# Modulation products on 32-column tiles of TensorE, and attention over 512 keys at a time, in a two-layer hybrid encoder

## The chip, the cores and the metric
The kernel runs on one core of a Trainium2 chip. The metric is the device time of one execution in microseconds (us). The engines are TensorE (PE; its weight loads are listed as PEld), VectorE (DVE), ScalarE (ACT), GpSimd (POOL) and SyncE (SP), which issues most of the transfers.

## The reference, cut to what matters
The program computes two layers over 1024 tokens of width 1024. Each sub-layer is a norm, a shift and scale that come from a vector c, the sub-layer itself, a gate from c, and a residual add. Layer 0 mixes the tokens by S5 blocks and stick-breaking attention side by side; layer 1 by two recurrences. A mixture of 32 experts follows each. The change touches the modulation (all twelve vectors of both layers are computed inside layer 0) and the attention:

```python
def modulate(h, shift, scale):
    return h * (1.0 + scale[:, None, :]) + shift[:, None, :]

def stick_breaking_attention(q, k, v):
    ...
        z = jnp.einsum('bhqd,bhkd->bhqk', q[:, :, s0:s1], k[:, :, :s1]).astype(jnp.float32) * scale
        mask = jnp.arange(s1)[None, :] < jnp.arange(s0, s1)[:, None]
        log_keep = jnp.where(mask, jax.nn.log_sigmoid(-z), 0.0)
        rc = lax.cumsum(log_keep, axis=3, reverse=True)
        suffix = jnp.concatenate([rc[..., 1:], jnp.zeros_like(rc[..., :1])], axis=-1)
        w = jnp.where(mask, jnp.exp(jax.nn.log_sigmoid(z) + suffix), 0.0)
        outs.append(jnp.einsum('bhqk,bhkd->bhqd', w.astype(v.dtype), v[:, :, :s1]))
```

Each modulation vector is silu(c) (1024 numbers) times a 1024 x 1024 matrix, plus a bias. There are eight heads of 64; queries come in blocks of 128.

## The kernel before, in words
A tile framework records the program and a scheduler places each instruction in its engine's queue; each engine and each transfer queue then works strictly in that order. The order is therefore not the order of the code.

`even` (L1970 on) is layer 0. Its stages in time: the first four token tiles are normed while `ada` computes scale1 and shift1; the norm's result is modulated and split into two parts (hTh, hTl) whose three products stand for one of full precision; eight weight tiles are loaded (`wl`), split (`wsplit`) and multiplied (`proj_u`, `proj_qk`, `proj_v`, by `mm3`, L240 to L242); then the loop over four S5 blocks (`s5_quad`) and eight attention blocks (`stick`) runs; then the gated unit `glu`, the output rows (`out_rows`) and the routing (`out_route`). The expert weights (L941) are loaded by numbers that the routing computes.

`ada` (L142) computes a modulation vector. A matrix comes in four loads of 1 MB into a ring of weight buffers. VectorE multiplies each of the eight row groups of a load by its 128 values of silu(c) and adds them up (L160, L167), which leaves one sum per partition and column; TensorE then adds over the partitions by products with a column of ones (L179). One load of the first vector goes to TensorE in whole (L177). Two vectors are computed at the start, eight between the projections (the `todo` list) and two in the gated unit. The ring has four buffers; two serve the projections' weights and two the modulation's (`pick`).

`stick(i)` (L283) computes 128 queries against (i+1) x 128 keys, for four pairs of heads, in blocks of 256 keys from the last to the first. Per block: two matmuls for the scores (L297), two sigmoids by ScalarE, on the block that holds the diagonal two masks by GpSimd (L307), then a running product over the keys from the right, by a scan per head on VectorE (L313) whose start is copied from the block before (L311), a product by GpSimd (L315), transposes by TensorE, an eviction (L322) and the value matmuls (L326):

```python
for r in range(2):
    v.tensor_tensor_scan(P[:, r, 0:n][:, ::-1], keep[:, r, 0:n][:, ::-1], zero.to_broadcast([128, n]),
                         P[:, r, n:n + 1], op0=OP.mult, op1=OP.add)
g.tensor_tensor(w[:, :, 0:n], w[:, :, 0:n], P[:, :, 1:n + 1], op=OP.mult)
```

Of the kernel before, what the change touches and what calls it, by code (L numbers as in the profile page):

```python
# [21 lines left out]
D = 1024  # L22
# [14 lines left out]
class Core:  # L37
# [42 lines left out]
    def consts(self):  # L80
        nc, c = self.nc, self.const
        ji = c.tile([128, 128], I32, name="ji")
        nc.gpsimd.iota(ji, pattern=[[1, 128]], base=0, channel_multiplier=-1)
        self.ident = c.tile([128, 128], FT, name="ident")
        nc.vector.tensor_scalar(self.ident, ji, 0.0, None, op0=OP.is_equal)
        self.ustrict = c.tile([128, 128], BF, name="ustrict")
        nc.vector.tensor_scalar(self.ustrict, ji, 0.0, None, op0=OP.is_gt)
        self.ones_b = c.tile([128, 128], BF, name="ones_b")
# [12 lines left out]
        nc.scalar.activation(self.cs, cr, AF.Silu)  # L101
        self.mod_d = self.dram.tile([2, 6, D], FT, name="mod_d")
# [39 lines left out]
    def ada(self, i, names, pool, tag, on_pe=((),), pool_eng=False):  # L142
# [4 lines left out]
        for m, nm in enumerate(names):  # L147
# [5 lines left out]
            for h in range(4):  # L153
                w = self.wload(aw[i, :, j * D + h * 256:j * D + (h + 1) * 256], 8)
                if h in on_pe[m % len(on_pe)]:
                    parts.append(w)
                    continue
                acc = pool.tile([128, 256], FT, name="adacc", bufs=4)
                eng = nc.gpsimd if pool_eng else nc.vector
                eng.tensor_scalar(acc, w[:, 0, :], self.cs[:, 0:1], None, op0=OP.mult)  # L160
                for k in range(1, KD):
                    wk, ck = w[:, k, :], self.cs[:, k:k + 1]
                    if pool_eng:
                        eng.tensor_scalar(wk, wk, ck, None, op0=OP.mult)
                        eng.tensor_tensor(acc, acc, wk, op=OP.add)
                    else:
# [4 lines left out]
            for h, x in enumerate(parts):  # L171
                for q in range(2):
                    qs = slice(q * 128, (q + 1) * 128)
                    p = pc[:, 2 * h + q:2 * h + q + 1]
                    if h in on_pe[m % len(on_pe)]:
                        for k in range(KD):
                            nc.tensor.matmul(p, x[:, k, qs], self.cs[:, k:k + 1], start=(k == 0), stop=(k == KD - 1))  # L177
                    else:
                        nc.tensor.matmul(p, x[:, qs], self.ones_f[:, 0:1], start=True, stop=True)  # L179
# [103 lines left out]
    def stick(self, i, qT, kT, vt, sb, zero):  # L283
# [3 lines left out]
        W = 256  # L287
        py = self.psum("d")
        nkey = (i + 1) * 128
        for hp in range(4):  # L290
            prev = None
            blk = 0
            for s in reversed(range((nkey + W - 1) // W)):
                k0, n = s * W, min(W, nkey - s * W)
# [4 lines left out]
                keep = sb.tile([128, 2, W], FT, name="keep", bufs=4)  # L299
                nc.scalar.activation(keep[:, :, 0:n], pzz, AF.Sigmoid, scale=-0.125)  # L300
                w = sb.tile([128, 2, W], FT, name="sw", bufs=4)
                nc.scalar.activation(w[:, :, 0:n], pzz, AF.Sigmoid, scale=0.125)
                P = sb.tile([128, 2, W + 1], FT, name="sP", bufs=4)
                if prev is None:
                    for tl, fill in ((keep, 1.0), (w, 0.0)):
                        d = tl[:, :, n - 128:n]
                        g.affine_select(d, d, pattern=[[0, 2], [-1, 128]], compare_op=OP.is_gt, fill=fill,  # L307
                                        base=0, channel_multiplier=1)
                    v.memset(P[:, :, n:n + 1], 1.0)
                else:  # L310
                    v.tensor_copy(P[:, :, n:n + 1], prev[:, :, 0:1])  # L311
# [1873 lines left out]
```

## Time and profile before

| what | value |
|---|---|
| median of 3 runs | 3071.89 us (3069.78 to 3077.01) |
| the profiled execution's own time | 3069.93 us |
| its span on the core | 3068.1 us |
| mean granted TensorE clock | 0.902 |
| busy share of the span: PE, DVE, ACT, POOL | 87%, 58%, 37%, 27% |
| DVE products of the modulation (L167) | 161.1 us, 329 instructions |
| DVE scans of the attention (L313) | 132.9 us, 160 instructions |

The shares are means over a program whose stages have different limits, so they don't tell what a stage waits for. In a time line, a matmul's duration includes the time until its result is out, so its successor starts before it ends; the distance between two starts is its price. TensorE's clock has two levels, 1.2 and 2.4 GHz; a granted clock of 0.82 is a mean of the two over a stretch. A matmul of plain float32 operands appears as two records, one of the split operands as one.

### The profile page before, as it was taken

The numbers are of one execution on the slowest core, as the hardware profiler recorded it, in microseconds if no ns is written. First come the engines' busy times: TensorE is split into PE (matmuls) and PEld (weight loads), VectorE is DVE, ScalarE is ACT, GpSimd is POOL, SyncE is SP. The second block draws the span as 40 slices with busy tenths as digits, with TensorE's granted clock in tenths as the row PEclk, the third lists the DMA queues.
The fourth block names the chain that finished last, engine by engine and source line by source line (L and its number), as shares of the span: only waits on it lengthen the run. The fifth ranks groups of instructions, "written<-read, shape, count | busy, mean of one in ns | idle before, by whom it ended". The sixth has DMA issues, their size and how long they took to land. (4 is left out here: it accounts for less than half of the span.)

```text
span 3068.1 us, 39923 instructions
## 1 busy us (share of the span) xinstructions
PE 2656.4 (87%) x14357; PEld 1854.7 (60%) x14357; DVE 1792.6 (58%) x3211; ACT 1120.7 (37%) x1777; POOL 831.2 (27%) x1157
## 2 busy tenths in 40 slices
PE   4987688989699999995799999999978799998991
PEld 4776466647444466662677777777877444566660
DVE  7546999655633477664734555646547434556664
ACT  4311456432232345552433323323233223345451
POOL 5260755324211031101301533354105111111101
PEclk9998689989799999997898978886988799999996
DMA  8746220223588899997745322244443689999995
GB/s 279 178 124 198 63 59 15 90 68 105 211 338 324 351 368 407 376 389 256 260 138 176 110 77 78 67 121 103 107 125 119 242 348 365 369 362 396 388 385 239
DMA packets 345018, 672.82 MB, mean 219 GB/s; under 512 B 118591, under 2 KB 259935, under 8 KB 293104
## 3 DMA queue, kind: packets, MB, share of 16 engines
q1 hardware_dynamic: 272960, 611.23, 54.7%
q10 hardware_dynamic: 56752, 25.41, 3.0%
q0 software_dynamic: 15104, 33.58, 3.0%
q8 instruction: 115, 1.88, 0.3%
q14 instruction: 87, 0.71, 0.1%
HBM read 611.31 MB, written 79.79 MB: 225 GB/s over the span
## 5 line engine op out<-in xcount | busy, mean ns | idle before, releaser
L139 DVE TENSOR_TENSOR wlo<-w,whi 128x1024 fp32r<-128x1024 f32 x384 | 451.4, 1220 | 114.0 <-ACT whi L138 112.3
L138 ACT ACTIVATE whi<-w 128x1024 fp32r<-128x1024 f32 x384 | 390.5, 1054 | 237.1 <-PE ps_g L839 69.9
L240 PE MATMUL ps_b<-hTh,wh 128*128 128x512 f32 x608 | 259.3, 428 | 28.2 <-ACT cc L1382 12.5
L241 PE MATMUL ps_b<-hTl,wh 128*128 128x512 f32 x608 | 255.2, 420 | 0.0
L242 PE MATMUL ps_b<-hTh,wl 128*128 128x512 f32 x608 | 254.8, 419 | 0.0
L788 POOL DMA_INDIRECT xg<-h_d,tok x56 | 80.6, 1440 | 641.6 <-PE ps_t L106 617.1
L847 DVE TENSOR_TENSOR hs<-hs,ps_u 128x512 f32<-128x512 f32 x48 | 32.9, 685 | 263.3 <-PE ps_u L917 212.4
L794 POOL DMA_INDIRECT ye_d<-y,tab x48 | 71.9, 1497 | 421.8 <-DVE y L856 328.4
L167 DVE SCALAR_TENSOR_TENSOR adacc<-w,cs,adacc 128x256 f32<-128x256 f32 x329 | 161.1, 507 | 5.2
L139 DVE TENSOR_TENSOR wl<-w,wh 128x1024 fp32r<-128x1024 f32 x84 | 104.0, 1253 | 97.3 <-ACT wh L138 88.1
L240 PEld LDWEIGHTS ps_b<-hTh,wh 128*128 128x128 f32 x608 | 124.8, 206 | 55.9 <-ACT cc L1382 13.3
L846 ACT ACTIVATE hs<-ps_g 128x512 f32<-128x512 f32 x48 | 28.7, 598 | 325.0 <-PE ps_g L917 244.8
L313 DVE TENSOR_TENSOR_SCAN sP<-keep,sP,sbz 128x256 f32<-128x256 f32 (+1 forms) x160 | 132.9, 874 | 21.7 <-POOL keep L307 10.5
L917 PE MATMUL ps_g<-w,xh 128*64 128x512 f32 x512 | 143.5, 598 | 0.0
L133 POOL TENSOR_TENSOR rs<-rm,nhalf 128x1 f32<-128x1 f32 (+2 forms) x56 | 49.9, 892 | 344.9 <-DVE rm L131 293.2
L138 ACT ACTIVATE wh<-w 128x1024 fp32r<-128x1024 f32 x84 | 86.3, 1053 | 150.5 <-PE ps_b L241 132.4
L241 PEld LDWEIGHTS ps_b<-hTl,wh 128*128 128x128 f32 x608 | 124.7, 205 | 27.2 <-DVE hTl L139 0.3
L242 PEld LDWEIGHTS ps_b<-hTh,wl 128*128 128x128 f32 x608 | 123.9, 204 | 28.3 <-issue 0.4
L917 PE MATMUL ps_u<-w,xh 128*64 128x512 f32 x512 | 137.6, 595 | 0.0
L315 POOL TENSOR_TENSOR sw<-sw,sP 128x512 f32<-128x512 f32 (+1 forms) x80 | 101.1, 1265 | 132.6 <-DVE sP L313 57.3
L926 PE MATMUL ps_y<-w,hh 128*64 128x512 f32 x512 | 122.0, 598 | 2.2 <-ACT hh L921 2.2
L1699 POOL TENSOR_TENSOR T<-N,X 128x60 f32<-128x60 f32 (+24 forms) x248 | 87.1, 351 | 125.2 <-DMA N<-n_d 93.3
(709 smaller groups left out, 6177.9 us busy)
## 6 DMA issues: line engine op xcount, KB each, us to landing
w<-in_moe_w_gate_dram SPq DMA_DIRECT2D x128, 1024.0 KB, 14.7
w<-in_moe_w_up_dram SPq DMA_DIRECT2D x128, 1024.0 KB, 14.8
w<-in_moe_w_down_dram SPq DMA_DIRECT2D x128, 1024.0 KB, 13.4
w<-in_ada_w_dram SPq DMA_DIRECT2D x48, 1024.0 KB, 5.8
w<-in_odd_w_in_dram SPq DMA_DIRECT2D x26, 1024.0 KB, 5.7
cy<-ye_d SPq DMA_DIRECT2D x16, 1024.0 KB, 10.8
cx<-xm_d SPq DMA_DIRECT2D x29, 512.0 KB, 7.5
w<-in_even_w_in_dram SPq DMA_DIRECT2D x8, 1024.0 KB, 8.5
```

The source lines that it names most:

```text
L138: self.nc.scalar.activation(hi, x, AF.Copy)
L139: self.nc.vector.tensor_tensor(lo, x, hi.bitcast(FT), op=OP.subtract)
L167: eng.scalar_tensor_tensor(acc, wk, ck, acc, op0=OP.mult, op1=OP.add)
L240: nc.tensor.matmul(p, a[0], b[0], start=first, stop=False)
L241: nc.tensor.matmul(p, a[0], b[1], start=False, stop=False)
L242: nc.tensor.matmul(p, a[1], b[0], start=False, stop=last)
L313: v.tensor_tensor_scan(P[:, r, 0:n][:, ::-1], keep[:, r, 0:n][:, ::-1], zero.to_broadcast([128, n]), P[:, r, n:n + 1], op0=OP.mult, op1=OP ...
L315: g.tensor_tensor(w[:, :, 0:n], w[:, :, 0:n], P[:, :, 1:n + 1], op=OP.mult)
L788: nc.gpsimd.indirect_dma_start(out=xg, out_offset=None, in_=h_d[:], in_offset=bass.IndirectOffsetOnAxis(ap=tokc, axis=0), bounds_check=T - ...
L917: nc.tensor.matmul(ps[z][r], x[:, 4 * h + k, r], w[z][h][:, k, :], start=(h == 0 and k == 0), stop=(h == 1 and k == 3))
L926: nc.tensor.matmul(py[n][r], ht[:, f, r], w[2][f // 2][:, f % 2, two[n]], start=(f == 0), stop=(f == 3))
L1699: g.tensor_tensor(o, N[:, 0:j, j:j + 1].to_broadcast([128, j, w]), X[:, j:j + 1, c:8].to_broadcast([128, j, w]), op=OP.mult)
```

## The change
`ada` no longer uses VectorE for products. silu(c) is stored in a tile `csz` whose 32 columns per row group hold the values in the first and zeros in the others. Each row group k is multiplied by TensorE with these 32 columns as weights, into the partitions of column tile k mod 4; the two groups that share a tile are accumulated. Two loads fill one bank, which ScalarE evicts; the sums over partitions by ones remain. Eight of the vectors move from the projections into the loop over S5 and attention blocks, one ahead of each `stick`; all four ring buffers serve the projections' weights first, three loads ahead.

`stick` takes 512 keys at a time. On the diagonal block both heads are scanned by one instruction over 2(n+1) elements: a zero in `keep` and a one in the added operand `mid` between the heads restart the product. The product with the sigmoids, the transposes and the value matmuls stay at 256 keys. `keep` and `P` have two buffers instead of four, of double size, `sw` and `swT` three.

```diff
-                acc = pool.tile([128, 256], FT, name="adacc", bufs=4)
-                eng = nc.gpsimd if pool_eng else nc.vector
-                eng.tensor_scalar(acc, w[:, 0, :], self.cs[:, 0:1], None, op0=OP.mult)
-                for k in range(1, KD):
...
-                        eng.scalar_tensor_tensor(acc, wk, ck, acc, op0=OP.mult, op1=OP.add)
+            for h2 in range(2):
+                pa = self.psum(tag)
+                for h in (2 * h2, 2 * h2 + 1):
+                    w = self.wload(aw[i, :, j * D + h * 256:j * D + (h + 1) * 256], 8)
+                    for k in range(KD):
+                        q = 32 * (k % 4)
+                        nc.tensor.matmul(pa[q:q + 32, h % 2 * 256:h % 2 * 256 + 256], self.csz[:, k, :], w[:, k, :],
+                                         start=(k < 4), stop=(k >= 4), tile_position=(0, q))
+                acc = pool.tile([128, 512], FT, name="adacc", bufs=2)
+                nc.scalar.activation(acc, pa, AF.Copy)
...
-        W = 256
+        W = 512
...
+                keep, w, P = [sb.tile([128, 2 * (W + 1)], FT, name=x, bufs=b)[:, 0:2 * (n + 1)].rearrange("p (r n) -> p r n", r=2)
+                              for x, b in (("keep", 2), ("sw", 3), ("sP", 2))]
...
+                    for r in range(2):
+                        g.memset(keep[:, r, n:n + 1], float(r))
+                    x, y = (x.rearrange("p r n -> p (r n)")[:, ::-1] for x in (keep, P))
+                    v.tensor_tensor_scan(y, x, mid[:, W - n:W + n + 2][:, ::-1], 1.0, op0=OP.mult, op1=OP.add)
...
-                pick(0)
-                w = {0: wl(0)}
+                w = {n: wl(n) for n in range(3)}
...
-                    pick(1)
-                    for _ in range((0, 1, 1, 2, 2, 2, 0, 0)[n]):
-                        for x in late:
-                            list(x)
-                        i, nm = todo.pop(0)
-                        late = [self.ada(i, [nm], ap, "e")]
-                        next(late[0])
...
                     for i in si:
+                        for x in late:
+                            list(x)
+                        late = [self.ada(j, [nm], ap, "e") for j, nm in todo[:1]]
+                        todo = todo[1:]
+                        for x in late:
+                            next(x)
                         stick(i)
```

Three places show how the queues change. The first is the queue of SP in the projections (w: a ring buffer; u_d and u: the S5 inputs on their way through memory; g_d, yo: the S5 outputs). Before:

```order
L77 DMA w<-in_even_w_in_dram 128x8x256
L262 DMA u_d<-ut 1024x1x64
L77 DMA w<-in_ada_w_dram 128x8x256 x3
L77 DMA w<-in_even_w_in_dram 128x4x512 x2
L77 DMA w<-in_ada_w_dram 128x8x256 x4
L77 DMA w<-in_s_w_glu_dram 128x4x512
L77 DMA w<-in_ada_w_dram 128x8x256 x5
L77 DMA w<-in_s_w_glu_dram 128x4x512
L77 DMA w<-in_ada_w_dram 128x8x256 x10
L547 DMA u_2314<-u_d 32x4x128 x8
```

The same stretch after the change:

```order
L77 DMA w<-in_even_w_in_dram 128x8x256 x6
L255 DMA u_d<-ut 1024x1x64 x2
L77 DMA w<-in_even_w_in_dram 128x4x512
L255 DMA u_d<-ut 1024x1x64 x5
L77 DMA w<-in_even_w_in_dram 128x4x512
L255 DMA u_d<-ut 1024x1x64
L77 DMA w<-in_ada_w_dram 128x8x256 x4
L544 DMA u_1845<-u_d 32x4x128 x8
L580 DMA g_d<-yo 32x4x128 x4
```

The modulation's loads have left the projections but for four ahead of the first S5 input, and the gated unit's weights are no longer loaded here.

The second is VectorE's queue where the attention begins (adacc: the modulation's sums; hr, hi, bb, tp: tiles of an S5 block; sP: the scan's result). Before:

```order
L160 TENSOR_SCALAR adacc<-w,cs 128x256
L167 SCALAR_TENSOR_TENSOR adacc<-w,cs,adacc 128x256 x6
L160 TENSOR_SCALAR adacc<-w,cs 128x256
L180 TENSOR_TENSOR adao<-ps_e,adac 128x8
L167 SCALAR_TENSOR_TENSOR adacc<-w,cs,adacc 128x256 x8
L556 MEMSET hr 128x4
L557 MEMSET hi 128x4
L309 MEMSET sP 128x2 x4
L160 TENSOR_SCALAR adacc<-w,cs 128x256
L167 SCALAR_TENSOR_TENSOR adacc<-w,cs,adacc 128x256 x6
```

After the change:

```order
L143 TENSOR_TENSOR wl<-w,wh 128x1024 x10
L553 MEMSET hr 128x4
L554 MEMSET hi 128x4
L335 TENSOR_TENSOR bb_1733<-bl_1729,cfr 128x64
L335 TENSOR_TENSOR t_1735<-bl_1730,cfi 128x64
L335 TENSOR_TENSOR bb_1734<-bl_1730,cfr 128x64
```

The projections' splits are followed at once by the first S5 block's operations.

The third is TensorE's queue at the end of the attention (gyh, gyl, gwh, gwl: the gated unit's split operands; csz: the modulation's weights). Before, inside the gated unit:

```order
L240 MATMUL ps_e<-gyh_4979,gwh_4995 128x512
L241 MATMUL ps_e<-gyl_4980,gwh_4995 128x512
L242 MATMUL ps_e<-gyh_4979,gwl_4996 128x512
L326 MATMUL ps_d<-swT,v 64x128 x4
L106 MATMUL ps_a<-ident,sw 128x128 x4
L297 MATMUL ps_b<-kT,qT 128x256 x2
L240 MATMUL ps_e<-gyh_4985,gwh_4995 128x512
L241 MATMUL ps_e<-gyl_4986,gwh_4995 128x512
```

After the change, where the gated unit begins:

```order
L164 MATMUL ps_e<-w,csz 32x256 x8
L325 MATMUL ps_d<-swT,v 64x128 x4
L110 MATMUL ps_a<-ident,sw 128x128 x4
L291 MATMUL ps_b<-kT,qT 128x128 x2
L172 MATMUL ps_e<-ones_f,adacc 128x1 x4
L325 MATMUL ps_d<-swT,v 64x128 x4
L110 MATMUL ps_a<-ident,sw 128x128 x4
L325 MATMUL ps_d<-swT,v 64x128 x4
L110 MATMUL ps_a<-ident,sw 128x128 x2
L233 MATMUL ps_e<-gyh_4639,gwh_4663 128x512
L234 MATMUL ps_e<-gyl_4640,gwh_4663 128x512
```

Modulation products now stand among the last attention blocks, and the gated unit starts when their last score matmuls (L291) have been issued.

## Rows read from the trace of the kernel before
**Rows 1.** Busy time by stretch; each engine's busy us and instructions, then clock and transfers.
```profile
core 0: us, PE busy (x) PEld busy (x) DVE busy (x) ACT busy (x) POOL busy (x), PEclk, DMA share, GB/s
0.00:50.00 50.00, 22.35 (x97) 19.78 (x98) 34.20 (x75) 18.91 (x30) 28.67 (x21) 1.00 0.96 318
...
284.00:552.00 268.00, 198.21 (x1335) 139.73 (x1333) 246.66 (x436) 135.34 (x283) 157.18 (x149) 0.82 0.21 55
552.00:640.00 88.00, 81.91 (x452) 57.89 (x452) 57.07 (x95) 31.30 (x57) 23.13 (x23) 0.92 0.28 84
640.00:698.00 58.00, 49.58 (x215) 26.35 (x212) 25.68 (x40) 23.16 (x40) 15.84 (x25) 0.85 0.19 57
```
**Rows 2.** Time lines of DVE and PE ahead of the projections: start us, us, engine, line.
```profile
50.86 0.17 DVE L180 TENSOR_TENSOR shift<-ps_e,adac 128x8 f32<-128x8 f32 x1
...
60.40 1.22 PE L240 MATMUL ps_b<-hTh,wh 128*128 128x512 f32 x2 [9.58 <-ACT hTh L138]
```
**Rows 3.** Groups of PE, 60 to 285 us: busy us, mean ns, idle before.
```profile
L240 PE MATMUL ps_b<-hTh,wh 128*128 128x512 f32 x192 | 80.7, 423 | 15.7 <-ACT hTh L138 9.6 <-ACT c L383 3.6 <-ACT ut L261 2.5
...
L240 PE MATMUL ps_b<-wh,hTh 128*128 128x512 f32 x64 | 25.1, 395 | 0.0
L179 PE MATMUL ps_e<-ones_f,adacc 128*128 128x1 f32 x112 | 15.5, 253 | 9.0 <-DVE adacc L167 9.0
```
**Rows 4.** Time line of PE at the first and the last matmuls of the projections.
```profile
61.41 0.63 PE L241 MATMUL ps_b<-hTl,wh 128*128 128x512 f32 x1
...
283.74 0.39 PE L240 MATMUL ps_b<-wh,hTh 128*128 128x512 f32 x1
283.97 0.39 PE L241 MATMUL ps_b<-wl,hTh 128*128 128x512 f32 x1
...
284.51 0.70 PE L297 MATMUL ps_b<-kT,qT 64*128 64x256 f32 x2
```
**Rows 5.** Groups of DVE, 284 to 697 us.
```profile
L313 DVE TENSOR_TENSOR_SCAN sP<-keep,sP,sbz 128x256 f32<-128x256 f32 (+1 forms) x160 | 132.9, 874 | 21.7 <-POOL keep L307 10.5 <-ACT keep L300 9.8
L167 DVE SCALAR_TENSOR_TENSOR adacc<-w,cs,adacc 128x256 f32<-128x256 f32 x80 | 39.9, 520 | 0.6
L311 DVE COPY sP<-sP 128x2 f32<-128x2 f32 x48 | 19.0, 397 | 1.2 <-DVE sP L313 0.5
...
L160 DVE TENSOR_SCALAR adacc<-w,cs 128x256 f32<-128x256 f32 x11 | 6.9, 632 | 18.4 <-DMA w<-in_ada_w_dram 17.7 <-PE ps_e L179 0.7
```
**Rows 6.** The scan's line: durations in ns, least, median and most.
```profile
L313 DVE TENSOR_TENSOR_SCAN sP<-keep,sP,sbz x160: 448/736/1895, 309.5 to 668.1; 128x256 f32<-128x256 f32 x128, 128x128 f32<-128x128 f32 x32
```
**Rows 7.** Groups of POOL, ACT and PE in the attention, 284 to 697 us.
```profile
L315 POOL TENSOR_TENSOR sw<-sw,sP 128x512 f32<-128x512 f32 (+1 forms) x80 | 101.1, 1265 | 132.6 <-DVE sP L313 57.3 <-ACT sw L302 52.7 <-DVE sP L309 9.7
L307 POOL TENSOR_SCALAR_AFFINE_SELECT sw<-sw 128x256 f32<-128x256 f32 x32 | 26.5, 829 | 29.5 <-ACT sw L302 26.8 <-issue 2.2
...
L322 ACT ACTIVATE swT<-ps_a 128x512 f32<-128x512 f32 (+1 forms) x80 | 44.6, 558 | 124.6 <-PE ps_a L106 99.9 <-issue 7.1 <-DVE bb L338 6.5
...
L326 PE MATMUL ps_d<-swT,v 128*64 128x128 f32 x576 | 58.1, 324 | 14.6 <-ACT swT L322 14.1
```
**Rows 8.** Time lines of PE and PEld where two 64-column tiles alternate (layer 0's experts).
```profile
850.90 3.65 PE L917 MATMUL ps_g<-w,xh 128*64 128x512 f32 x16
854.38 2.74 PE L917 MATMUL ps_u<-w,xh 128*64 128x512 f32 x10
...
851.38 0.14 PEld L917 LDWEIGHTS ps_g<-w,xh 128*64 128x64 f32 x2 [0.29 <-issue]
```
**Rows 9.** Time line of PE at the first output rows and the first split output matmul.
```profile
684.61 3.60 PE L681 MATMUL ps_e<-w,gl 128*128 128x512 f32 x8
688.05 3.60 PE L681 MATMUL ps_e<-w,qT 128*128 128x512 f32 x8
...
698.49 0.79 PE L240 MATMUL ps_e<-wh,yh 128*128 128x512 f32 x1
```
**Rows 10.** Time line of SP's queue: the first expert weight.
```profile
805.11 0.37 SPq L941 DMA_DIRECT2D w<-in_moe_w_gate_dram  x1
```

More of the change, by code (lines that the diff above doesn't have):

```diff
@@ L146, in ada @@
         aw, ab = a["ada_w"], a["ada_b"]
-        for m, nm in enumerate(names):
+        for nm in names:
             j = order.index(nm)
@@ L170, in ada @@
             pc = self.psum(tag)
[L171 to L179, printed above, removed]
+            for n in range(KD):
+                nc.tensor.matmul(pc[:, n:n + 1], parts[n // 4][:, n % 4 * 128:n % 4 * 128 + 128], self.ones_f[:, 0:1], start=True, stop=True)
             nc.vector.tensor_tensor(o, pc[:, 0:KD], b, op=OP.add)
@@ L323, in stick @@
-                for b in range(nb):
-                    for r in range(2):
-                        h = 2 * hp + r
-                        nc.tensor.matmul(py[64 * r:64 * r + 64, hp * 128:(hp + 1) * 128], vt[:, s * 2 + b, h * 64:(h + 1) * 64],
-                                         wT[:, (r * nb + b) * 128:(r * nb + b + 1) * 128],
-                                         start=(blk == 0), stop=(blk == i))
-                    blk += 1
-                prev = P
+                    for r in range(2):
+                        v.tensor_tensor_scan(P[:, r, 0:n][:, ::-1], keep[:, r, 0:n][:, ::-1], mid[:, 0:1].to_broadcast([128, n]),
+                                             P[:, r, n:n + 1], op0=OP.mult, op1=OP.add)
@@ new lines, in stick @@
+                prev = P
+                for b0 in reversed(range(0, n // 128, 2)):
+                    m = min(2, n // 128 - b0)
+                    ks = slice(b0 * 128, (b0 + m) * 128)
+                    g.tensor_tensor(w[:, :, ks], w[:, :, ks], P[:, :, b0 * 128 + 1:(b0 + m) * 128 + 1], op=OP.mult)
+                    pt = self.psum("a")
+                    for r in range(2):
+                        for z in range(m):
+                            self.transpose(pt[:, (r * m + z) * 128:(r * m + z + 1) * 128], w[:, r, (b0 + z) * 128:(b0 + z + 1) * 128])
+                    wT = sb.tile([128, 512], FT, name="swT", bufs=3)
+                    nc.scalar.activation(wT[:, 0:256 * m], pt[:, 0:256 * m], AF.Copy)
+                    for z in range(m):
+                        b = k0 // 128 + b0 + z
+                        for r in range(2):
+                            h = 2 * hp + r
+                            first = k0 + n == nkey and b0 + 2 >= n // 128 and z == 0
+                            nc.tensor.matmul(py[64 * r:64 * r + 64, hp * 128:(hp + 1) * 128], vt[:, b, h * 64:(h + 1) * 64],
+                                             wT[:, (r * m + z) * 128:(r * m + z + 1) * 128],
+                                             start=first, stop=(k0 == 0 and b0 == 0 and z == m - 1))
@@ L2092, in even @@
                     for i in si:
+                        for x in late:
[4 more added lines that the diff above has]
+                            next(x)
                         stick(i)
+                for x in late:
+                    list(x)
             phasors.close()
```

72 lines of the change are left out of this document (23 added, 49 removed).

## The prediction
> **What bounds the kernel now.** I read the busy table by stretches first [rows 1], then the time lines at the seams of the first layer [rows 2, 9, 10], then the groups of instructions inside each stretch. Only the first layer up to its routing is touched. The first expert weight is issued at 805.11 us [rows 10], on a queue whose issue waits for the routing result, and everything behind hangs on that. So what the first 805 us lose or gain moves the end of the program one for one, give or take the second layer's reordering. Four stretches matter. **Start:** the modulation vector is ready at 50.86 us and the first projection matmul starts at 60.40 [rows 2]. **Projections:** 60.4 to 284.5 us [rows 2, 4], the stretch of the big matmuls, where TensorE should run freely and, as worked out below, doesn't. **Attention with the S5 blocks:** from 284 to 552 us VectorE is busy 246.7 of 268 us, 92%, while TensorE's clock is granted at 0.82: VectorE bounds it. **Gated unit and first output rows:** 552 to 698.5 us, no engine alone; the gated unit is woven into the last attention blocks, and the first split output matmul comes at 698.49 [rows 9].
>
> **Start (gain 9 us).** Eight weight loads of 1 MB feed the first two modulation vectors. Today VectorE multiplies seven of them, in a chain that ends with the last product shortly before 50.9. On TensorE the products no longer limit; the loads do. The queue must land 11.5 MB (six x tiles and a seventh, eight weights) before the last product. At the 318 GB/s of this stretch [rows 1] that is 36 us; 2 us of matmuls, one eviction, eight column sums and an add follow, near 4 us together. That is 40 instead of 50.9. I take 9, with bounds 3 (loads stretched by waits for the ring) and 12.
>
> **Projections (gain 31 us).** The 768 large matmuls (six groups, three of 192 and three of 64, one of each shown [rows 3]) start 0.23 us apart when nothing interrupts [rows 4]: 175 us. With 24 transposes (5 us) that makes 180 of the 224.1 us; 44 are lost. Of these, the 112 small column sums take about 13 us (15.5 of overlapping duration), waits for VectorE's product sums 9.0 [rows 3], other waits about 8, and the rest, 14 us, is the lower of the two clock levels, 1.2 instead of 2.4 GHz, at which TensorE is found behind such gaps: the third matmul after the wait before 60.40 lasts 0.63 us, one in a long run 0.39 [rows 2, 4]. The change takes the sums, their waits and about 9 us of slow clock out of this stretch: 31 us. Bounds: 14 if only waits and part of the sums go, 40 if all but the other waits go. VectorE's splits for the projections become free of a neighbour, and four ring buffers instead of two prefetch the weights; I cost both at nothing, since TensorE hides them.
>
> **Attention, gated unit, output (gain 68 us).** Today 284.5 to 698.5, 414 us. *VectorE.* Removed: modulation products 39.9 + 6.9 us; 32 of 48 one-column copies at 0.40 us, 12.7 [rows 5]; the memsets go to GpSimd. The scans: 160 instructions become 64 over the same 36,900 elements. From the medians of 0.736 us for 256 and the minimum 0.448 for 128 [rows 6], an element costs 2.25 ns and an instruction 0.16 us. So 64 scans take 93 us undisturbed, and 114 with the stretch that today's sum shows (132.9 against 108). That removes 19 to 40 us. Together 79 to 100 us of durations; as durations overlap by about 6%, some 75 to 95 of the 329 busy us in 284 to 698. About 214 us are left for attention and S5. *GpSimd* keeps 101 us of products and 48 of masks (one of their two rows shown) [rows 7], with some 45 for S5 and 64 one-column memsets: about 200. *ScalarE* saves on 32 fewer pairs of sigmoids and gains sixteen evictions of the size of today's 0.56 [rows 7]. *TensorE* keeps its attention work and gains eight modulations of 32 products. A 512-column product of two records takes 0.86 us (eight records in 3.44 us [rows 9]), so one of 256 columns 0.43. If four 32-column tiles run side by side, 256 of them cost 27 us; one after another, 110. The nearest row has two 64-column tiles: sixteen records in 3.48 us, 0.22 each, half of 0.43 [rows 8]. So tiles do run side by side, and I take 27.
>
> That makes three engines of 200 to 225 us, where today one of 247 set the pace. I therefore don't carry over VectorE's 92%; at 80% attention takes 214 / 0.80 = 268 us. The order puts the gated unit behind the last attention blocks instead of among them: 192 matmuls at 0.23 us, 44, plus 2 for its start. Then 64 records of output rows at 0.43 us [rows 9] with 4 for a slow start, 32. Sum 346 against 414. Bounds: 92% busy gives 233 and a gain of 103; TensorE with the serial price is the first rival.
>
> The rows show the weights of the paired tiles loaded in 0.14 us per pair inside a period of 0.43 [rows 8], while TensorE never stands still: the loads are hidden. The Trainium skill, "TensorE: Matmul & The Clock Gate", Part 3 (The mechanism), says a weight load overlaps running matmuls only when its row group differs; column tiles share theirs. By that rule 512 loads would add 0.07 us each, an estimate of 36 us of TensorE in the attention, and my sum would end about 20 us later, near 2984. The row contradicts it, so my sum goes by the row.
>
> The Trainium skill, "TensorEngine Tiling (Array Packing)", Key Properties, says that changing the tiling mode drains the engine. Some 50 changes, each at most the difference between a transpose's 0.33 us and its turn of 0.11, would be 11 us by that rule. It is spread over an engine that has that room here, and no row shows a drain by itself.
>
> **What could be late next.** The ring holds exactly one modulation's four weights, so each next load waits for TensorE to pass the product before it; behind it on the queue of SP stand the S5 inputs of the next block and, late, the gated unit's inputs and weights. I cost this at nothing, since the transfer queue is used to a fifth in this stretch [rows 1]; the cover is the 268 us of attention for 32 MB (100 us at the rate of the start). The keep and scan buffers shrink from four of 256 to two of 512 keys; that is the third case below.
>
> **Sum.** 9 + 31 + 68 = 108 us off the profiled execution's own 3069.9 us (span 3068.1 and 1.8 around it): 2962. The median of the runs is 2 us above that execution, so 2964.
>
> **Rivals.** *First: the 32-column tiles run one after another.* For it: no row shows four of them. Against it: the pair of rows 8. TensorE would have 198 us (284 to 552) plus a quarter of 178 (the three attention groups, one shown [rows 7]) plus 110, 352 us, and become the bound: 430 with gated unit and output, 16 worse than today there, and with the 40 of the first stretches 24 us faster: 3048. *Second: the engines overlap as today.* VectorE at 92% and the start at its best give 12 + 31 + 103: 2926. For it: GpSimd and VectorE slow each other less when the products are gone (a scan runs up to 1.895 us against 0.736 [rows 6]). Against it: GpSimd and TensorE have no slack to lend. *Third, slower: the chain of a block sets the pace.* A block of 512 keys goes through two pairs of matmuls (1.7 us), two sigmoids (about 1.1 each), two masks (0.7 and 0.8), a scan of 1026 elements (2.5), a product (1.3), transposes, eviction and value matmuls (0.6 each): near 10.5 us. With two keep buffers two blocks can be in flight, 5.2 us each, and 48 blocks need 252 us, inside my 268. Break-even with today lies at 414 + 40 - 78 = 376 us, 7.8 us a block. If only one block is under way at a time, it is 504 us: 128 slower, near 3200. For it: fewer, larger blocks and halved buffers, with two masks and two memsets in series on GpSimd ahead of the scan. Against it: S5 work and another head pair's block stand between on every queue.
>
> **How the numbers follow.** Forecast with its own spread 0.78; first rival 0.10; second 0.07; third 0.05. The range reaches to 2918 (second rival with 8 us of reordering in the second layer) and to 3008 (half of the serial price, smallest gains ahead). Above it lie the first and third rivals. About 0.2% is what a measurement can tell from no change: faster 0.92, same 0.03, slower 0.05.
>
> **What would show it.** Right: projections' first matmul near 50 us and attention's first near 245; modulation products starting about 0.11 us apart; VectorE below 90% in the attention; first split output matmul near 590; first expert load near 697. Wrong: product matmuls 0.2 us apart or more (first rival), VectorE above 90% (second), GpSimd or ScalarE waiting in turn for the scan with every engine under 70% (third), or the seam at 805 moved while the end did not.

## The result, and the profile after the change

The change makes the kernel slower: 3120.66 us (median of 4 runs, 3110.23 to 3126.25) against 3071.99, a ratio of 1.0151 with the interval 1.0122 to 1.018. Forecast was 2964. The profiled execution has a span of 3108.5 us.

Busy time by stretch of the changed kernel, to be read beside [rows 1]:

```profile
core 0: us, PE busy (x) PEld busy (x) DVE busy (x) ACT busy (x) POOL busy (x), PEclk, DMA share, GB/s
0.00:50.00 50.00, 24.51 (x200) 14.89 (x200) 8.13 (x25) 22.09 (x37) 32.43 (x23) 0.80 1.04 343
...
55.00:243.00 188.00, 183.08 (x797) 149.82 (x799) 38.31 (x123) 46.53 (x60) 57.84 (x178) 0.97 0.16 46
243.00:400.00 157.00, 113.09 (x855) 75.32 (x855) 112.38 (x153) 71.69 (x129) 99.22 (x133) 0.86 0.32 73
400.00:500.00 100.00, 75.64 (x545) 49.07 (x547) 59.53 (x75) 50.60 (x86) 52.49 (x61) 0.82 0.33 100
500.00:610.00 110.00, 86.89 (x762) 57.98 (x758) 51.20 (x64) 49.68 (x83) 41.63 (x56) 0.86 0.64 166
610.00:718.00 108.00, 95.89 (x465) 62.25 (x461) 28.92 (x39) 24.18 (x38) 7.01 (x13) 0.93 0.50 139
```

VectorE's busy time in the attention is 223 us, near the 214 that were forecast, but that is 61% of 367 us where 80% of 268 was forecast, and 92% before: the attention got longer all the same. No engine is at 90% there; TensorE, the busiest, has 276 us (75%). The time line of PE shows the seams (first projection matmul, first score matmul L291, gated unit, output rows, first split output matmul), and the products L164 among the last attention blocks:

```profile
55.17 1.22 PE L233 MATMUL ps_b<-hTh,wh 128*128 128x512 f32 x2 [10.97 <-ACT hTh L142]
...
242.87 0.70 PE L291 MATMUL ps_b<-kT,qT 64*128 64x256 f32 x4
...
542.67 2.77 PE L164 MATMUL ps_e<-w,csz 128*32 128x256 f32 x48
545.38 0.65 PE L325 MATMUL ps_d<-swT,v 128*64 128x128 f32 x6
...
556.09 1.94 PE L164 MATMUL ps_e<-w,csz 128*32 128x256 f32 x16 [6.09 <-DMA w<-in_ada_w_dram]
...
559.84 1.13 PE L291 MATMUL ps_b<-kT,qT 64*128 64x512 f32 x4
560.90 1.07 PE L164 MATMUL ps_e<-w,csz 128*32 128x256 f32 x16
561.90 0.66 PE L325 MATMUL ps_d<-swT,v 128*64 128x128 f32 x8
...
610.83 0.79 PE L233 MATMUL ps_e<-gyh,gwh 128*128 128x512 f32 x1
...
684.25 0.68 PE L678 MATMUL ps_e<-w,gl 128*128 128x512 f32 x1
...
718.03 0.48 PE L233 MATMUL ps_e<-wh,yh 128*128 128x512 f32 x1
```

Beside [rows 2, 4, 9]: the start gained 5.2 us (60.40 to 55.17), the projections 36.4 (224.1 to 187.7). The stretch from the first score matmul to the first split output matmul, the **attention stretch** below, grew from 414.0 to 475.2. The queue of SP, beside [rows 10]:

```profile
542.92 0.39 SPq L77 DMA_DIRECT2D w<-in_ada_w_dram  x1
...
569.10 20.05 SPq L77 DMA_DIRECT2D w<-in_ada_w_dram  x6
592.36 2.54 SPq L77 DMA_DIRECT2D w<-in_s_w_glu_dram  x2
...
825.81 0.37 SPq L938 DMA_DIRECT2D w<-in_moe_w_gate_dram  x1
```

The first expert weight comes 20.7 us later, the end of the span 40.4 us. The gated unit's weights are issued at 592.36, behind the modulation's loads, and its first matmul at 610.83 stands behind the last scores, not among the attention blocks.

Groups of PE from 243 to 718 us: the products are 45.0 us (ten vectors, two of them in the gated unit) and wait 18.8 for loads; the value matmuls wait 36.5 for ScalarE's evictions, 14.1 before [rows 7].

```profile
L325 PE MATMUL ps_d<-swT,v 128*64 128x128 f32 x576 | 57.5, 317 | 37.4 <-ACT swT L319 36.5 <-issue 0.6
...
L164 PE MATMUL ps_e<-w,csz 128*32 128x256 f32 x640 | 45.0, 414 | 18.8 <-DMA w<-in_ada_w_dram 18.8
...
L172 PE MATMUL ps_e<-ones_f,adacc 128*128 128x1 f32 x160 | 20.5, 253 | 0.8 <-ACT adacc L167 0.8
```

Groups of DVE in the same stretch, the scans, 93.1 us in place of 132.9 [rows 5]:

```profile
L303 DVE TENSOR_TENSOR_SCAN sP<-keep,sbm 128x514 f32<-128x514 f32 (+3 forms) x32 | 52.7, 1646 | 59.7 <-POOL sw L313 23.4 <-POOL keep L301 18.1 <-POOL keep L298 18.1
L307 DVE TENSOR_TENSOR_SCAN sP<-keep,sP,sbm 128x512 f32<-128x512 f32 x32 | 40.4, 1301 | 6.2 <-ACT keep L293 5.3
```

The waits of 243 to 610 us (who waits for whom, us, times, longest) go in a circle. VectorE waits for GpSimd, GpSimd for ScalarE, ScalarE for VectorE, and ScalarE and TensorE wait for each other:

```profile
ACT swT L319 <- PE ps_a L110: 67.8, 46, 6.8
...
PE ps_d L325 <- ACT swT L319: 36.5, 15, 8.9
...
POOL sw L313 <- ACT sw L294: 24.4, 6, 11.9
...
DVE sP L303 <- POOL sw L313: 23.4, 4, 8.4
ACT keep L293 <- DVE sP L303: 18.2, 8, 4.5
```

### The profile page after: what moved, and what is told of

The parts are those of the page before. It is cut to its first block, busy times and chain, and to the rows that moved or that the text cites. A ratio compares the mean times of both kernels' runs of the same rounds, so it can differ in the third digit from the quotient of the medians.

```text
span 3108.5 us, 40569 instructions
## 1 busy us (share of the span) xinstructions
PE 2688.3 (86%) x14969; PEld 1854.8 (60%) x14969; DVE 1585.6 (51%) x2678; ACT 1129.0 (36%) x1735; POOL 810.9 (26%) x1223
## 3 DMA queue, kind: packets, MB, share of 16 engines
q1 hardware_dynamic: 272960, 611.23, 53.5%
## 5 line engine op out<-in xcount | busy, mean ns | idle before, releaser
L785 POOL DMA_INDIRECT xg<-h_d,tok x56 | 73.2, 1308 | 658.0 <-PE ps_t L110 624.6
L110 PE MATMUL ps_t<-ident,xg 128*128 128x128 f32 (+1 forms) x448 | 75.6, 307 | 42.5 <-DVE wlo L143 31.3
L836 PE MATMUL ps_g<-wlo,xh 128*128 128x512 f32 x256 | 105.3, 411 | 7.8 <-DVE wlo L143 7.6
```

The source lines that it names most:

```text
L110: self.nc.tensor.transpose(out, in_, self.ident[:n, :n])
L836: nc.tensor.matmul(p, x[a][:, k, :], w(b, j)[:, ns], start=(first and a + b == 0), stop=(last and a == 1))
```

## The experiments

The seams of every profiled execution. "Stretch" is the attention stretch, behind it TensorE's and VectorE's busy time in it; the median stands beside that of the kernel before from the same session.

| run | first projection | first score | stretch | PE, DVE busy | first expert | median (before) |
|---|---|---|---|---|---|---|
| before | 60.4 | 284.5 | 414.0 | 330, 329 | 805.1 | 3072.0 |
| changed | 55.2 | 242.9 | 475.2 | 372, 252 | 825.8 | 3120.7 (3072.0) |
| e1 | 54.3 | 242.1 | 483.3 | 379, 296 | 833.2 | 3124.5 (3075.5) |
| e2 | 59.9 | 282.9 | 416.5 | 328, 303 | 806.1 | 3093.5 (3075.5) |
| e3 | 54.2 | 330.0 | 384.0 | 316, 249 | 820.5 | 3097.3 (3075.5) |
| e4, e4 again | 54.2 | 284.5 | 379.6 | 314, 250 | 770.6 | 3053.6 (3075.5) |
| e5 | 54.8 | 242.5 | 437.5 | 362, 251 | 786.9 | 3521.7 (3069.3) |
| e6 | 55.2 | 288.9 | 380.7 | 321, 259 | 776.0 | 3054.7 (3069.3) |
| e9 | 55.3 | 244.3 | 481.7 | 377, 258 | 833.1 | 3091.8 (3069.3) |
| e10 | 60.4 | 283.1 | 385.3 | 319, 277 | 774.8 | 3060.4 (3069.3) |
| e12 | 59.9 | 283.8 | 432.5 | 337, 322 | 822.9 | 3117.5 (3073.8) |
| e12b | 60.4 | 283.6 | 419.0 | 335, 318 | 809.0 | 3080.1 (3073.8) |
| e13 | 55.3 | 278.1 | 409.3 | 327, 327 | 793.9 | 3086.8 (3073.8) |
| l0_before | 60.2 | 288.2 | 421.7 | 331, 329 | 816.6 | 1492.5 (3082.7) |
| l0_after | 54.8 | 241.8 | 485.7 | 376, 253 | 834.7 | 1514.4 (3082.7) |
| f1 | 53.5 | 241.1 | 496.0 | 360, 356 | 844.2 | 3158.5 (3082.7) |
| f3 | 54.4 | 303.8 | 400.9 | 314, 286 | 811.4 | 3108.5 (3082.7) |
| g1 | 55.6 | 279.2 | 410.2 | 328, 323 | 796.1 | 3070.9 (3071.0) |
| g2 | 55.2 | 242.6 | 481.9 | 383, 271 | 831.5 | 3108.7 (3071.0) |

In the row of e4 the median is that of e4, the rest is from e4 again. The first layer of l0_before has the rows of before in the same order, and its stretch took 421.7 instead of 414.0; l0_after 485.7 instead of 475.2. Differences of a stretch under some 10 us say nothing. Nor does a whole time tell of the first layer, since the scheduler orders the second anew at nearly every edit.

TensorE's busy share of the stretch lies between 77 and 84% in every run but f1 (73%), VectorE's between 52 and 80%. The stretch follows TensorE's busy time more closely than VectorE's. That is seen across runs and shows no cause by itself; the experiments below move the work.

**One half of the change each.** e1 is the changed kernel with `stick` as before; e2 is the kernel before with the new `stick`:

```diff
-    def stick(self, i, qT, kT, vt, sb, zero):
...
-        W = 256
+    def stick(self, i, qT, kT, vt, sb, mid):
...
+        W = 512
```

> The modulation products on TensorE inside the attention, as in the changed kernel, but the attention at 256 keys with a scan per head and four buffers, as before. Theory A (place): the eight vectors stand in TensorE's queue of the attention, wait there for their loads and hold the gated unit's weights back; the 512 keys cost nothing. Then this run is as slow as the changed kernel, 3100 to 3140 us, and the stretch from the first score matmul to the first split output matmul stays at 450 to 490 us (475 in the changed kernel, 414 before). Theory B (blocks): 512 keys with two buffers instead of four make the chain of a block the pace; the products are harmless. Then that stretch falls to 350 to 400 us and the run takes 3000 to 3050 us.

> The attention at 512 keys with one scan on the diagonal, as in the changed kernel, but the modulation on VectorE between the projections, as before. Theory A (place): VectorE is relieved of some 30 us of scans and copies and TensorE gets nothing new: faster than before by 10 to 40 us, 3030 to 3062 us. Theory B (blocks): slower than before by 20 us or more, 3092 us and above, with the stretch from the first score matmul to the first split output matmul above 440 us.

The stretch was 483 with the products alone and 416.5 with the 512 keys alone: the loss belongs to the modulation's move, as theory A has it. But by theory A e2 was to be faster, and the 26 us of busy time that VectorE loses there bought nothing. Its median, 3093.5, is in theory B's range and slower by 0.7% (interval 0.5 to 0.9%), though its stretch is far under theory B's 440 and its first expert weight is at 806.1: that loss lies behind the first layer.

**The eight vectors elsewhere, or nowhere.** e3 puts them back between the projections, on TensorE. e4 leaves out their loads, products and sums.

```diff
-                        late = [self.ada(j, [nm], ap, "e") for j, nm in todo[:1]]
...
+                    for _ in range((0, 1, 1, 2, 2, 2, 0, 0)[n]):
...
+                        late = [self.ada(i, [nm], ap, "e")]
```

```diff
-            for h2 in range(2):
+            for h2 in range(0 if skip else 2):
```

> The changed kernel with the eight vectors put back between the projections (two buffers of the ring for them, two for the projections' weights, as before), still multiplied by TensorE. Theory A (place): the attention loses its products and the gated unit is woven into it again: its stretch falls from 475 to 380 to 410 us, the projections grow from 188 to about 215 to 235 us; 3010 to 3060 us. Theory B (blocks): the attention's stretch stays above 440 us and the run at 3100 us or more.

> The changed kernel without the loads, products and sums of the eight vectors in the attention (these vectors hold only their biases; that part of the computation is left out). It prices them: Theory A (place) expects the stretch from the first score matmul to the first split output matmul to fall from 475 to 350 to 380 us and the run to 2990 to 3030 us; Theory B (blocks) expects it to stay above 430 us, the run above 3070 us.

> The same kernel as in e4 (the eight vectors hold only their biases), for its profile. It tells what the attention with 512 keys takes with no modulation in it: e3, which has none there but the last two, measured 384 us from the first score matmul to the first split output matmul. If products, sums and loads of the eight are the whole excess, it is 375 to 395 us; the products alone (e5, 437.5) then cost some 50 us and the loads 38. If it is above 420, something else than the eight vectors holds the attention.

384.0 and 379.6 us: without modulation the attention takes 380. In e3 the projections grew to 275.8 us, 88 more than in the changed kernel and beyond the 235 expected, and the run took 3097.3 where 3010 to 3060 was expected: on TensorE the work costs there too. On VectorE, as before, it costs the projections 36 (224.1 against 187.7), and the attention stretch some 32 (e2 against e3), in which VectorE still multiplies eleven loads. The stretch of e4 in one row (columns as in the first view): TensorE is busy for 83% of it, VectorE for 66%.

```profile
284.50:664.10 379.60, 313.97 (x1983) 208.88 (x1982) 250.16 (x317) 186.76 (x319) 197.75 (x262) 0.91 0.19 57
```

Its whole time is no price, since its projections take 230 us, for another reason. With nothing ahead of them, the eight biases are copied early in VectorE's queue and wait there for their loads (waits of DVE, 55 to 130 us):

```profile
DVE adao L171 <- DMA adac<-in_ada_b_dram: 34.6, 5, 18.7
```

**Products or loads.** e5 multiplies the keys, which lie on the chip, instead of loaded weights; e6 loads the weights and leaves the products out.

```diff
-                    w = self.wload(aw[i, :, j * D + h * 256:j * D + (h + 1) * 256], 8)
...
+                        w = res[:].rearrange("p a (b n) -> p (a b) n", n=256)
```

```diff
+            if skip:
+                for h in range(4):
+                    self.wload(aw[i, :, j * D + h * 256:j * D + (h + 1) * 256], 8)
-            for h2 in range(2):
+            for h2 in range(0 if skip else 2):
```

> The changed kernel with all products and sums of the eight vectors in the attention, but multiplied with data that lie on the chip already (the keys), so that their 32 loads of 1 MB are left out (these vectors come out as other numbers). The attention's stretch (first score matmul to first split output matmul) is 475 us in the changed kernel. Theory P (the products and sums themselves fill TensorE's queue): it stays at 450 to 475 us. Theory L (the loads: TensorE waits in order for each, and the gated unit stands behind the last of them): it falls to 400 to 430 us, and the gated unit's products start before the last score matmuls again.

> The converse: the 32 loads of the eight vectors stay in the attention, their products and sums are left out (these vectors hold only their biases). Theory P expects the attention's stretch at 390 to 420 us; Theory L, so far as the loads' place on the transfer queue is meant and not TensorE's wait for them, at 445 us or more.

```profile
242.50:680.00 437.50, 362.36 (x2623) 240.62 (x2622) 250.63 (x327) 198.26 (x336) 193.13 (x262) 0.88 0.19 50
```

This row is the stretch of e5. Products and sums alone add 58 us to 380 (theory P gave 450 to 475, theory L 400 to 430: it lies between; the gated unit starts at 548.6, ahead of the last scores, as L has it). TensorE is busy 48 us more than in e4 and idle 10 us more. But e5 has idle time of its own, 25 us of waits for coefficients of the S5 blocks, which take 4 in e4 and in the changed kernel (the first row; the second belongs to what follows):

```profile
PE ps_e L110 <- DMA cl<-in_s_c_im_dram: 22.6, 4, 7.4
PE ps_d L328 <- ACT swT L322: 11.5, 14, 3.2
```

So the 58 is rather high as a price, and the split between products and loads is good to some 20 us. The other 38 come with the loads: 28 of them are idle time of TensorE (103 us in the changed kernel, 75 in e5), which waits there for the loads (18.8) and longer for ScalarE's evictions (36.5 against 11.5). But leaving the loads out also brings the gated unit's weights forward, to 138 us, and its matmuls back among the attention blocks; how much of the 38 that is stays open. e6 tells less than it was meant to: nothing paces its 32 loads, so all were issued by 289 us, ahead of the attention, and it only shows the stretch without the vectors once more. Its stretch is under both ranges. The whole times of e4, e5 and e6 can't be compared with the others: their vectors hold other numbers, on which the routing depends, and in e5 the extra time lies behind a first expert weight that comes early (786.9).

**Earlier in the attention.** e9 puts two vectors ahead of each of the first four blocks.

```diff
-                        late = [self.ada(j, [nm], ap, "e") for j, nm in todo[:1]]
+                        for _ in range(2):
...
+                            late = [self.ada(j, [nm], ap, "e") for j, nm in todo[:1]]
```

> The changed kernel with two of the eight vectors ahead of each of the first four attention blocks instead of one ahead of each of eight, so that all are done before the last blocks. Theory L in its form that the last vectors hold the gated unit back: its first product comes before the last score matmuls, the stretch falls from 475 to 430 to 455 us, the run to 3075 to 3105 us. Theory P: the work is the same, so the stretch stays at 465 to 480 us and the run at 3110 to 3125 us.

Stretch 481.7, gated unit at 611.8: unchanged, as theory P has it. The condition of theory L was met, with little room: the gated unit's weights are issued at 529, and its first product stands 12 us ahead of the last scores (624.3). TensorE's waits for loads grew, from 18.8 to

```profile
PE ps_e L164 <- DMA w<-in_ada_w_dram: 33.1, 15, 7.0
```

That its ratio is 1.0064 and not 1.0151 comes from behind the first layer.

**Is VectorE the bound?** e10 leaves out half the scans of the kernel before.

```diff
-                for r in range(2):
+                for r in range(1):
                     v.tensor_tensor_scan(P[:, r, 0:n]
```

> The kernel before with one scan per block instead of two; both heads of a pair are multiplied with the first head's products (half of the running products are left out). VectorE loses some 66 us of its 329 between 284 and 698 us. If VectorE bounds that stretch, as the prediction had it, the stretch shrinks from 414 to 350 to 375 us and the run to 3010 to 3040 us. If TensorE's queue with its waits sets the pace (theory T), it shrinks by under 20 us: 395 to 414, and the run stays at 3050 to 3080 us.

```profile
283.10:668.40 385.30, 319.39 (x1999) 216.59 (x1998) 276.81 (x487) 188.37 (x380) 184.76 (x196) 0.88 0.24 67
```

The same row of the kernel before (VectorE 329 busy us) is

```profile
284.50:698.50 414.00, 329.71 (x1999) 224.04 (x1998) 328.95 (x569) 189.80 (x380) 196.15 (x196) 0.84 0.23 62
```

VectorE is busy 52 us less and the stretch is 29 shorter: between the two expectations. A microsecond of relief on VectorE is worth about half of one here, between 0.4 and 0.75 with the spread of 10 us.

**The blocks.** e12 is e2 at 256 keys with four buffers, e12b the same with the changed kernel's numbers of buffers. The first lines show e12 against e2, the second e12b against e12.

```diff
-        W = 512
+        W = 256
```

```diff
-                              for x, b in (("keep", 4), ("sw", 4), ("sP", 4))]
+                              for x, b in (("keep", 2), ("sw", 3), ("sP", 2))]
```

> The kernel before with both heads of a pair in one scan on the diagonal block, still 256 keys at a time and four buffers; modulation as before. In e2 (512 keys, two buffers) VectorE lost some 40 us of scans and copies and the stretch stayed at 416.5 us, while leaving out 66 us of scans in e10 gave 29 back. Theory B (512 keys and two buffers ate what the relief gave): here the relief is some 10 us (32 scans fewer at 0.16 us, 16 fewer waits) and nothing is eaten: 400 to 412 us, the run 3055 to 3070. Theory S (the single scan over two heads delays both, and is itself the loss): 416 us or more.

> As e12, with the buffers of the changed kernel (two for the factors and the scan's result, three for the rest) but of 256 keys. If the number of buffers is what ate the relief in e2, the stretch is 10 to 40 us longer than in e12; if it is the size of the blocks, the two agree within 5 us.

432.5 and 419.0: neither is faster than before, and fewer buffers are not slower. So at 256 keys the halved number of buffers costs nothing. Whether the single scan costs something (theory S) can't be told from these: 18.5 us is more than the 10 between executions, but e12b has the same scan and is within it. Two buffers of 512 keys remain a rival for what ate e2's relief: more of them have no room beside the S5 tiles, and that wasn't tried. VectorE waits for GpSimd's product, which reads the scan's result, for 34 us in the changed kernel (the 23.4 shown above and the row below), 9 in e2 and 1 in the kernel before and in e12b:

```profile
DVE sP L305 <- POOL sw L313: 10.6, 5, 3.7
```

**The engine or the place?** f1 is the changed kernel with the eight vectors at the same place, multiplied by VectorE.

```diff
+                    nc.vector.tensor_scalar(x, w[:, 0, :], self.cs[:, 0:1], None, op0=OP.mult)
+                    for k in range(1, KD):
+                        nc.vector.scalar_tensor_tensor(x, w[:, k, :], self.cs[:, k:k + 1], x, op0=OP.mult, op1=OP.add)
```

> The changed kernel with the eight vectors at the same place in the attention and with the same loads, but multiplied by VectorE as before (some 130 us there: 256 instructions of 0.51 us); TensorE keeps only their sums over partitions. Theory T (TensorE's queue sets the pace, VectorE has room at 252 of 475 us): the attention's stretch falls from 475 to 420 to 450 us. Theory V (VectorE bounds as soon as it is filled; 250 + 130 of 380): 450 to 480 us.

```profile
241.10:737.10 496.00, 360.34 (x2109) 241.73 (x2109) 355.81 (x552) 187.32 (x319) 211.36 (x262) 0.79 0.37 102
```

496 us, against 485.7 of the changed first layer on the same chip: above both ranges, and theory T falls as it stood. VectorE is busy for 72% and the stretch is no shorter. TensorE's granted clock is 0.79 in this row, against 0.85 in l0_after's stretch; what that adds was not separated. In this stretch the work costs on either engine.

**What the second layer adds.** The two kernels cut after the first layer (`ODD = False`):

> The kernel before with the second layer left out (final norm right after the first layer), as a base for the next run: some 1420 us for the first layer and its experts, and 10 to 40 for the end.

> The changed kernel with the second layer left out. If the change costs what the seam at the first expert weight shows (805.1 to 825.8 us) and the rest of the 49 us is the second layer's new order, it is 15 to 27 us above the same cut of the kernel before. If the first layer's experts or its end lose too, it is 35 us or more above it.

1492.5 and 1514.4: the change costs 21.9 us there, as the seam says; the other 27 of the 49 us arise behind it. g2 moves two small operations to VectorE, after which most rows behind the first layer stand as before:

```diff
-                nc.scalar.activation(acc, pa, AF.Copy)
+                nc.vector.tensor_copy(acc, pa)
...
-            nc.gpsimd.memset(mid, 0.0)
+            nc.vector.memset(mid, 0.0)
```

> The changed kernel with two small operations moved to VectorE (the clearing of the scan's added operand, the eviction of the products), after which the scheduler gives the rows behind the first layer almost the order of before. If the second layer's order is the rest of the loss, it is 15 to 30 us slower than before (3087 to 3102) instead of 49; if not, 40 us or more.

3108.7, ratio 1.0128 (1.011 to 1.0147): 38 us slower than before instead of 49, with overlapping intervals, and between the two expectations. In the profiled executions g2 loses 26 us up to the first expert weight and 6 behind it, the changed kernel 21 and 20. So the new order looks like most of what is lost behind the seam, but the differences are near the spread.

**Versions that the findings point to.** e13 takes only the first two vectors to TensorE; g1 six of their eight loads, which leaves every row from the experts on as before; f3 adds to e13 the 512 keys and the last two vectors between the projections.

```diff
-                    list(self.ada(0, ["scale1", "shift1"], ap, "e", ((2,), ())))
+                    list(self.ada(0, ["scale1", "shift1"], ap, "e", tiles=True))
...
+                    list(self.ada(0, ["scale1", "shift1"], ap, "e", ((),), tiles=((0,), (0, 1))))
...
+                        late = [self.ada(i, [nm], ap, "e", tiles=len(todo) < 2)]
```

> The kernel before with only the first two vectors, those the projections wait for, multiplied on 32-column tiles; the other ten stay on VectorE, the attention as before. Both theories give the start's gain alone: the first projection matmul at 54 to 56 instead of 60.4 us, the first expert weight at 799 to 802 instead of 805.1, and 3060 to 3070 us if the second layer keeps its order.

> The kernel before with 32-column tiles for six of the first eight loads of the modulation (the other two stay on VectorE) and nothing else changed; all rows of the second layer and of the experts stand as before on every engine. In e13 (eight of eight) the first layer came out 11 us earlier and the run 12 us later, with a second layer in another order. If that order is the price, this run is 4 to 12 us faster than before (about 3060 to 3068 against 3072). If the order is harmless and something else was slow in e13, it is 5 us or more slower than before.

> 512 keys and the products on 32-column tiles for four vectors alone: the first two, which the projections wait for, and the last two of those between the projections, which VectorE carried into the attention before; the other six stay on VectorE (the last two vectors of all too, in the gated unit). Theory T: first projection matmul at 55, attention's stretch 380 to 395 us, first expert weight at 780 to 790 instead of 805.1 us. If the second layer keeps its pace, 3045 to 3055 us; its order alone moved other runs by up to 28 us either way, so up to 3080.

e13 and g1 have the first expert weight 11 and 9 us earlier, and neither is faster: 3086.8, slower by 0.5% (0.3 to 0.7%), and 3070.9 with a ratio of 0.9999 (0.9988 to 1.0009). f3 lost 25 us in the projections to its two vectors and missed its ranges: stretch 400.9, first expert weight at 811.4, 3108.5 us. g1 is instructive. Up to 2013 us it is 11 us ahead; by the second layer's experts nothing is left. Two of the stretches between, first before, then g1, cut at the same transfers:

```profile
2024.30:2056.40 32.10, 29.50 (x242) 23.36 (x243) 13.89 (x28) 7.64 (x17) 7.79 (x22) 0.79 0.53 121
2137.10:2185.00 47.90, 46.68 (x429) 38.75 (x429) 23.15 (x48) 15.65 (x44) 5.49 (x5) 0.90 0.30 65
```

```profile
2013.00:2050.10 37.10, 33.49 (x242) 26.48 (x243) 13.94 (x29) 7.65 (x17) 9.64 (x28) 0.68 0.44 106
2131.90:2183.80 51.90, 50.09 (x429) 41.48 (x429) 23.82 (x49) 15.63 (x44) 5.50 (x5) 0.83 0.23 61
```

The same 242 and 429 matmuls take 5 and 4 us longer at a granted clock of 0.68 instead of 0.79 and 0.83 instead of 0.90. Order alone is therefore not the whole of what happens behind the first layer; how much it is of the change's 27 us stays open.

## Why the prediction was wrong, point by point

**Start, −9: right in kind.** Measured −5.2, inside 3 to 12. The shift vector came at 44.2 us, not 40.

**Projections, −31: right.** Measured −36.4, inside 14 to 40; TensorE is busy for 183 of 188 us and the granted clock is 0.97. It is the modulation's move that did it: e1 has 187.8 us there, e2 without the move 223.0.

**Price of a product and of a scan: right.** 48 records in a row take 2.71 us (542.67 to 545.38), 0.113 a product where 0.11 was forecast: the four tiles run side by side, and the first rival falls. The Trainium skill, "TensorE: Matmul & The Clock Gate", Part 3 (The mechanism), says that a weight load overlaps running matmuls only when its row group differs. By that rule a product would take 0.25 us, an estimate from 0.11 and two loads of 0.07; the row decides against it here. The Trainium skill, "TensorEngine Tiling (Array Packing)", Key Properties, says that a change of the tiling mode drains the engine. A drain is at most 0.1 us here: a group of 16 records between others takes 1.00 us (560.90 to 561.90) where 16 of the 48 take 0.90. The scans came to 93.1 us, where 93 to 114 were forecast.

**Attention, −68: wrong, measured +61.2.** The step that failed is "three engines of 200 to 225 us, where today one of 247 set the pace", with the 268 us of attention at 80% of VectorE that follow from it. In the prediction's own terms, attention took 368 us instead of 268 (242.87 to 610.83), the gated unit 73 instead of 46 and the output rows 34 instead of 32.

The figure for TensorE was wrong on the prediction's own rows. Its first rival counts 198 us plus a quarter of 178 for TensorE without the products; with 27 for the products that is 270, not 200 to 225. The column sums, 16 us here (128 records at 0.128), are in neither. Measured were 276 us of TensorE, more than the whole 268: even with no wait at all the forecast could not have held.

The reading behind the step had two halves. *VectorE bounds it*: half true at most by e10 (52 busy us less, 29 gained) and e2 (26 less, nothing beyond the spread). *The others have room for what is added*: shown false by e4, e5 and the changed kernel. By the experiments, the miss of 129 us (475 against 346) has these terms, each with the spread of some 10 us:

- attention without the eight vectors, gated unit and output rows: 380 instead of 346, +34, although the gated unit is woven into the attention in e4, which the forecast did not assume;
- products and sums of the eight: 58 instead of nothing. On TensorE they are 48 us (e5 against e4), so little of it was hidden: some 10 us, if e5's own waits are left out;
- loads: 38 instead of the nothing that "What could be late next" gave them. The transfer queue had room (its share is 0.32 to 0.64); 28 of the 38 are idle time of TensorE. What the gated unit's later place adds to it was not separated.

The third rival named a chain through all queues and was the nearest, but it hung it on halved buffers, which e12b speaks against at 256 keys and which no run tested at 512, and gave it 0.05. After these runs the 92% reads as that of one engine in a ring of four that wait for each other, not as that of a bound. That reading was not tested by itself.

**The gated unit: wrong.** It was put at 46 us behind the attention and took 73 (610.83 to 684.25), with two vectors in it: TensorE spends 14 us on their products and sums and waits 8.5 for their loads.

**"Moves the end of the program one for one, give or take the second layer's reordering": wrong in the give or take.** The seam at the first expert weight moved by 20.7 us, the end by 40.4, the medians by 49; 8 us of reordering were allowed for.

## What to carry to other kernels

In a stage where several in-order queues wait for each other, a busy share tells neither the bound nor the room: add up each engine's work in the new order first, then leave the work out, or move it alone, and read the seams. Here a microsecond taken from VectorE gave about half of one, and one added to TensorE's queue cost about a whole one, the wait for its load besides. Judge an edit at a seam, and run an unrelated edit too: a scheduler that reorders everything behind it moves a whole time by as much as the edit.

## What was not expected of the hardware

Four 32-column tiles of plain float32 operands take 0.056 us a record of 256 columns, where one after another would be an estimate of 0.215 (half of 0.43 [rows 9]): nearly four times as fast, and the price of a product on TensorE was not what failed. And the same order of instructions was granted another TensorE clock in the same two stretches of two kernels (0.68 against 0.79, 0.83 against 0.90), and with it went 9 of the 11 us by which g1 was ahead. Over all runs of that session the mean granted clock of the whole kernel was 0.895 on average for g1 and 0.899 for the kernel before, so it is hardly one execution's chance.
